# A block's output projection by seven products of quarters, with prepared weights kept in DRAM

## The chip, the cores and the metric

The kernel runs on one core of one Trainium2 chip. The metric is the device time of one execution in microseconds, median of several. TensorE is called PE here, VectorE DVE, ScalarE ACT, GpSimd POOL, and SyncE, which issues nearly all DMAs, SP.

## The reference

One layer on x of 1024 tokens by 1024 channels, all in float32. Two attentions of 8 heads each (a and b) run on one normed input; each is gated, projected to 1024 channels, weighted by its own sigmoid gate, and the sum goes through one output projection that is added to x with a gate per channel:

```python
merged = (jax.nn.sigmoid(mg_a) * (y_a @ w_branch_a[l])
          + jax.nn.sigmoid(mg_b) * (y_b @ w_branch_b[l]))
x = x + gate[:, None, :] * (merged @ w_out[l])
```

`merged` is 1024 x 1024, `w_out` 1024 x 1024; `gate` has one value per output channel and comes from c alone.

## The kernel before

Every product is made in three passes: both operands are split into a high part (rounded, ACT) and a low part (the rest, DVE), and high x high, high x low and low x high are summed in one accumulator (`mm3`, lines 129 to 132). All engines' orders are written by hand: the tile framework keeps program order on each engine and adds the waits. SP's queue is in order too: a DMA that waits holds all that follow.

Places in SBUF are slots of two pools: 29 of 4 KB a partition (`U`) and 11 of 2 KB (`Hs`), handed out oldest first (lines 42 to 72). A slot may be given out while its last readers still run; the new writer then waits for them.

The attention (lines 1239 to 1296) runs 16 heads (0 to 7 branch a, 8 to 15 branch b) of 12 steps each. A step turns one column block of p by PE transposes into a bank `pt` (two banks, shared with the transposes that prepare q and k), ACT casts the high part and DVE takes the low part (lines 1192, 1193), and the product with v is queued for the next step (line 1295). Between them stand the scores of the next blocks (row maximum on DVE, exponential on ACT, scaling by the inverse sum on POOL, lines 1143 to 1178), the preparation of the next pair of heads, a list `extra` of calls at given steps (line 1287), and then filler matmuls (lines 909 to 1013) until PE's planned time of the step is used up. The fillers are the gates' products and, in heads 14 and 15 and after them, the branch products: per 128 channels and 512 tokens 12 matmuls, then DVE's evacuation (lines 984 to 999) to `mA`, whose high and low parts go into `hT_hi` and `hT_lo` as the projection's left operand. One filler chunk's weights are loaded when the chunk before it starts, behind what line 1010 has asked for, and split one unit later.

`w_out` is loaded in two halves of columns (2 MB each): the first when branch a's products end (line 1010), split on ACT and POOL during branch b's (line 1012); the second before `output` and split inside it. `output` (lines 1299 to 1332) makes 16 tiles of 128 tokens x 512 channels, 24 matmuls each; DVE multiplies by the gate row spread over all partitions, adds x, and the tile is stored. The last tile is made in two halves of 256 columns. `gate_row` (line 894) puts the gate into DRAM in head 3.

## Time and profile before

| | us |
|---|---|
| median of 3 runs | 975.56 (973.75 to 977.09) |
| profiled execution | 970.98 |
| its span, first to last instruction | 969.0 |
| attention, heads 4 to 11 | about 428 to 687 |
| branch a's, then b's products end | about 832 and 876 |
| output projection, PE | 877.6 to 965.1 |

The granted TensorE clock was 0.998 of full speed over the span. Busy time of PE counts pipelined matmuls and says when it had work, not its peak rate; a stretch in which PE is busy throughout can get longer only by waits. How far apart matmuls start is the rate.

### The profile page before, as it was taken

The numbers are of one execution on the slowest core, as the hardware profiler recorded it, in microseconds if no ns is written. First come the engines' busy times: TensorE is split into PE (matmuls) and PEld (weight loads), VectorE is DVE, ScalarE is ACT, GpSimd is POOL, SyncE is SP. The second block draws the span as 40 slices with busy tenths as digits, with TensorE's granted clock in tenths as the row PEclk, the third lists the DMA queues.
The fourth block names the chain that finished last, engine by engine and source line by source line (L and its number), as shares of the span: only waits on it lengthen the run. The fifth ranks groups of instructions, "written<-read, shape, count | busy, mean of one in ns | idle before, by whom it ended". The sixth has DMA issues, their size and how long they took to land.

```text
span 969.0 us, 15332 instructions
## 1 busy us (share of the span) xinstructions
PE 952.2 (98%) x5582; PEld 832.3 (86%) x5582; DVE 636.0 (66%) x1379; ACT 477.6 (49%) x959; POOL 204.0 (21%) x260
## 2 busy tenths in 40 slices
PE   7999999999999999999999999999999999999998
PEld 7999999999988888788888888888888878887887
DVE  3967977787646667567667676677676766596222
ACT  7776634443245656546555566465655644143000
POOL 0022132200011222122233233232332220045000
PEclk9999999999999999999999999999999999999999
DMA  9821132864943224225232232322411554633321
GB/s 348 322 95 45 50 116 81 295 225 169 312 134 98 87 67 131 66 74 155 79 109 67 66 90 67 114 85 88 132 56 44 185 185 153 245 141 125 109 88 66
DMA packets 80987, 124.99 MB, mean 129 GB/s; under 512 B 5928, under 2 KB 47536, under 8 KB 80912
## 3 DMA queue, kind: packets, MB, share of 16 engines
q1 hardware_dynamic: 80912, 124.01, 39.3%
q8 instruction: 44, 0.72, 0.3%
q14 instruction: 31, 0.25, 0.1%
HBM read 88.33 MB, written 35.66 MB: 128 GB/s over the span
## 4 chain that ended last, share of the span: by engine, by line
PE 89%; DVE 4%; DMA 3%; ACT 2%; issue 2%; POOL 0%; SPq 0%; ACTq 0%; DVEq 0%
PE f L127 31%; PE b L127 12%; PE out L127 9%; PE s L127 9%; PE o L127 7%; PE pt L136 6%; PE q L127 3%; PE ckv L127 2%; PE kv L127 2%; PE cq_s L127 2%; DVE hT_lo L998 1%; DMA ks_u<-ka_d 1%; PE cq_t L127 1%; DVE mg_h L991 1%; PE pada L127 1%
## 5 line engine op out<-in xcount | busy, mean ns | idle before, releaser
L1192 ACT CAST pp_u<-pt 128x512 fp32r<-128x512 f32 x192 | 92.2, 480 | 178.9 <-PE pt L136 164.9
L1193 DVE TENSOR_TENSOR pp_u<-pt,pp_u 128x512 fp32r<-128x512 f32 x192 | 106.5, 555 | 76.5 <-ACT pp_u L1192 74.4
L127 PE MATMUL f<-hT_hi,hi_f_u 128*128 128x512 f32 x384 | 153.9, 401 | 0.0
L127 PE MATMUL f<-hT_lo,hi_f_u 128*128 128x512 f32 x384 | 153.7, 400 | 0.0
L127 PE MATMUL f<-hT_hi,lo_f_u 128*128 128x512 f32 x384 | 153.5, 400 | 0.0
L127 PE MATMUL s<-k_u,q_u 96*128 96x512 f32 (+6 forms) x480 | 117.1, 363 | 1.2 <-ACT p_h L1172 0.7
L127 PE MATMUL b<-hi_b_u,hT_hi 128*128 128x256 f32 x384 | 109.6, 286 | 0.0
L127 PE MATMUL b<-hi_b_u,hT_lo 128*128 128x256 f32 x384 | 108.6, 283 | 0.0
L127 PE MATMUL b<-lo_b_u,hT_hi 128*128 128x256 f32 x384 | 108.6, 283 | 0.0
L1176 POOL TENSOR_SCALAR p_u<-p_u,rs 128x640 f32<-128x640 f32 (+1 forms) x64 | 64.7, 1011 | 169.1 <-DVE rs L1175 93.2
L1166 DVE TENSOR_REDUCE nm<-s 128x1 f32<-128x128 f32 (+7 forms) x128 | 97.0, 758 | 4.4
L127 PE MATMUL o<-pp_u,v_u 128*128 128x512 f32 (+7 forms) x384 | 94.4, 340 | 0.0
L1176 POOL TENSOR_SCALAR p_h<-p_h,rs 128x128 f32<-128x128 f32 (+1 forms) x64 | 36.9, 577 | 249.3 <-DVE rs L1175 220.0
L127 PEld LDWEIGHTS s<-k_u,q_u 96*128 96x128 f32 (+2 forms) x480 | 77.1, 191 | 7.0 <-ACT p_h L1172 1.2
L127 PEld LDWEIGHTS f<-hT_hi,lo_f_u 128*128 128x128 f32 x384 | 72.5, 189 | 12.0
L127 PEld LDWEIGHTS f<-hT_hi,hi_f_u 128*128 128x128 f32 x384 | 72.7, 189 | 11.1
L127 PEld LDWEIGHTS f<-hT_lo,hi_f_u 128*128 128x128 f32 x384 | 72.5, 189 | 11.2
L127 PEld LDWEIGHTS o<-pp_u,v_u 128*128 128x128 f32 (+1 forms) x384 | 62.0, 162 | 19.7 <-issue 0.2
L127 PEld LDWEIGHTS b<-lo_b_u,hT_hi 128*128 128x128 f32 x384 | 73.6, 192 | 0.3
L127 PEld LDWEIGHTS b<-hi_b_u,hT_hi 128*128 128x128 f32 x384 | 73.6, 192 | 0.3
L127 PEld LDWEIGHTS b<-hi_b_u,hT_lo 128*128 128x128 f32 x384 | 73.6, 192 | 0.0
L136 PEld LDWEIGHTS pt<-ident,p_u 128*128 128x128 f32 x416 | 52.7, 140 | 16.7
(310 smaller groups left out, 1998.5 us busy)
## 6 DMA issues: line engine op xcount, KB each, us to landing
raw_f_u<-in_w_t SPq DMA_DIRECT2D x24, 512.0 KB
wada_u<-in_w_ada SPq DMA_DIRECT2D x16, 512.0 KB
mg_d<-th_h SPq DMA_DIRECT2D x32, 256.0 KB
mg_h<-mg_d SPq DMA_DIRECT2D x32, 256.0 KB
raw_b_u<-in_w_b SPq DMA_DIRECT2D x12, 512.0 KB
x_u<-in_x SPq DMA_DIRECT2D x8, 512.0 KB
raw_wg_u<-in_w_gate SPq DMA_DIRECT2D x8, 512.0 KB
va_d<-vhl_u SPq DMA_DIRECT2D x8, 512.0 KB
```

The source lines that it names most:

```text
L127: self.nc.tensor.matmul(out, lhsT=l, rhs=r, start=start, stop=stop)
L136: self.nc.tensor.transpose(out=out, in_=in_, identity=self.ident)
L991: nc.vector.scalar_tensor_tensor(out=m, in0=m, scalar=1.0, in1=acc, op0=ALU.add, op1=ALU.mult)
L998: nc.vector.tensor_tensor(out=self.hT_lo[x], in0=mA[c1][:, x[2]], in1=self.hT_hi[x].bitcast(F32), op=ALU.subtract)
L1166: nc.vector.tensor_reduce(out=nm, in_=sv, axis=AX.X, op=ALU.max, negate=True)
L1176: nc.gpsimd.tensor_scalar(out=p[:, 0:w], in0=p[:, 0:w], scalar1=rs, scalar2=0.0, op0=ALU.mult, op1=ALU.add)
L1192: nc.scalar.copy(ph[:, c0:], pt[:, c0:])
L1193: nc.vector.tensor_tensor(out=pl[:, c0:], in0=pt[:, c0:], in1=ph[:, c0:].bitcast(F32), op=ALU.subtract)
```

## The change

Operands and result of the output projection are cut into quarters: A11, A12 (channels 0 to 511 and 512 to 1023 of the first 512 tokens), A21, A22 (of the last 512 tokens), and B11 to B22 of `w_out`, already multiplied by the gate. Seven products of quarters (Winograd's form of Strassen's scheme) take the place of eight:

- the left operands are A11, A11 - A21, A12, S2 = S1 - A11, S1 = A21 + A22, A22 and S4 = A12 - S2; the right ones, in the same order, are B11, T3 = B22 - B12, B21, T2 = B22 - B12 + B11, T1 = B12 - B11, T4 = B21 - T2 and B22;
- the four quarters of the result are sums of the products, made on DVE, and x is added; the gate multiplication of the result is gone;
- S1, S2 and S4 are made on DVE from the float32 `mA`, which is now kept, and split into the places of quarters of `hT_hi` and `hT_lo` that are no longer needed. A11 - A21 is made in the branch products, in place of A21 itself (four more DVE steps of 128 x 512).

The right operands are made in heads 4 to 11, one group of rows in each two heads (k = 0 to 3): two loads of 512 KB of `w_out` and one of the gate row at steps 0 and 1, the gate multiplication at steps 4 and 6, and then seven parts, at steps 8 and 10 of the even head and 1, 3, 5, 7, 9 of the odd one. Each part is up to two sums, one cast on ACT, one subtraction on DVE; its high and low parts (256 KB each) are stored to DRAM at the next part. All seven are 14 MB. `wo_load` reads one of them back as four DMAs of 512 KB: 11 and T3 when branch a's products end, the other five during `output`.

```diff
-        low, mA = [], {}
+        low, mA = [], self.mA
...
                     mf = mA[c][:, sl]
                     nc.vector.scalar_tensor_tensor(out=m, in0=m, scalar=1.0, in1=acc, op0=ALU.add, op1=ALU.mult)
                     nc.vector.tensor_tensor(out=mf, in0=mf, in1=m, op=ALU.add)
+                    if sh and c < 4:
+                        mf = Hs.get([P, 512], F32, f"dA{c}")
+                        nc.vector.tensor_tensor(out=mf, in0=mA[c][:, 0:512], in1=mA[c][:, 512:1024], op=ALU.subtract)
                     nc.scalar.copy(self.hT_hi[:, c, sl], mf)
-                    low.append((c, sh))
+                    low.append((c, sh, mf))
                     while len(low) > (pos + 1 < len(todo)):
-                        c1, s1 = low.pop(0)
+                        c1, s1, m1 = low.pop(0)
                         x = (slice(None), c1, slice(s1 * 512, s1 * 512 + 512))
-                        nc.vector.tensor_tensor(out=self.hT_lo[x], in0=mA[c1][:, x[2]], in1=self.hT_hi[x].bitcast(F32),
-                                                op=ALU.subtract)
-                        if s1:
-                            U.put(mA.pop(c1))
+                        nc.vector.tensor_tensor(out=self.hT_lo[x], in0=m1, in1=self.hT_hi[x].bitcast(F32), op=ALU.subtract)
+                        if s1 and c1 < 4:
+                            Hs.put(m1)
...
-                    self.w_out_load(0)
-            if kind == 1 and sh == 1 and c in (2, 3, 4, 5):
-                self.w_out_split(0, c - 2)
...
-    def w_out_split(self, c, k):
-        self.wo[c][k] = self.split(self.wo[c][k], f"wo{c}{k}", engine=self.nc.gpsimd)
...
+    WO = ("11", "21", "22", "T1", "T2", "T3", "T4")
+
+    def gate_bc(self):
+        self.gbc = self.U.get([P, D], F32, "gbc")
+        self.nc.sync.dma_start(self.gbc, self.gate_d.broadcast_to([P, D]))
+
+    def wo_rows(self, k):
+        self.wr = [self.load_w(self.t["w_out"][k + 4 * e], [P, 2, 512], f"wo{k}{e}") for e in range(2)]
+
+    def wo_gate(self, e):
+        self.nc.vector.tensor_tensor(out=self.wr[e], in0=self.wr[e], in1=self.gbc.rearrange("p (a b) -> p a b", a=2),
+                                     op=ALU.mult)
+        if e:
+            self.U.put(self.gbc)
+
+    def wo_store(self):
+        for dst, x in self.wo_pending:
+            self.nc.sync.dma_start(dst, x.bitcast(F32))
+            self.Hs.put(x)
+        self.wo_pending = []
+
+    def wo_part(self, k, name):
+        nc, Hs = self.nc, self.Hs
+        self.wo_store()
+        (b11, b12), (b21, b22) = ((x[:, 0], x[:, 1]) for x in self.wr)
+        tmp = None
+        if name[0] == "T":
+            tmp = Hs.get([P, 512], F32, f"w{name}{k}")
+            a, b = {"T1": (b12, b11), "T3": (b22, b12), "T2": (b22, b12), "T4": (b21, self.t2)}[name]
+            nc.vector.tensor_tensor(out=tmp, in0=a, in1=b, op=ALU.subtract)
+            if name == "T2":
+                nc.vector.tensor_tensor(out=tmp, in0=tmp, in1=b11, op=ALU.add)
+        x = {"11": b11, "21": b21, "22": b22}.get(name, tmp)
+        hi, lo = (Hs.get([P, 512], F32R, f"w{name}{k}{e}") for e in "hl")
+        nc.scalar.copy(hi, x)
+        nc.vector.tensor_tensor(out=lo, in0=x, in1=hi.bitcast(F32), op=ALU.subtract)
+        i = self.WO.index(name)
+        self.wo_pending = [(self.wo_d[i, e, :, k], y) for e, y in enumerate((hi, lo))]
+        if name == "T2":
+            self.t2 = tmp
+        elif tmp is not None:
+            Hs.put(tmp)
+        if name == "T4":
+            Hs.put(self.t2)
+
+    def wo_done(self):
+        self.wo_store()
+        self.U.put(*self.wr)
+
+    def wo_load(self, name):
+        i = self.WO.index(name)
+        out = []
+        for h in range(2):
+            pair = [self.U.get([P, 2, 512], F32R, f"w{e}{name}{h}") for e in "hl"]
+            for e, x in enumerate(pair):
+                self.nc.sync.dma_start(x.bitcast(F32), self.wo_d[i, e, :, 2 * h:2 * h + 2])
+            out.append(pair)
+        self.wo[name] = out
...
+        order = [(st, 0) for st in range(4)] + [(st, 1) for st in range(4, 8)] + [(st, 0) for st in range(4, 8)] + \
+            [(st, 1) for st in range(4)]
...
+        def sum_a(dst, a, b, op):
+            for k in range(4):
+                nc.vector.tensor_tensor(out=dst(k), in0=a(k), in1=b(k), op=op)
+
+        def split_a(src, k0, cols):
+            for k in range(4):
+                nc.scalar.copy(hi[:, k0 + k, cols], src(k))
+            for k in range(4):
+                nc.vector.tensor_tensor(out=lo[:, k0 + k, cols], in0=src(k), in1=hi[:, k0 + k, cols].bitcast(F32),
+                                        op=ALU.subtract)
+
+        s1f = lambda k: mA[k][:, R]
+        s2f = lambda k: mA[k][:, L]
+        s4f = lambda k: mA[4 + k][:, L]
...
+        def banks(tags):
+            out = []
+            for tag in tags:
+                b = self.bank(tag, f"out_{tag}{len(out)}")
+                out += [b[:, 0:512], b[:, 512:1024]] if tag == "s" else [b]
+            return out
+
+        def product(acc, k0, tok, name, ls=slice(0, 512)):
+            for k in range(4):
+                wh, wl = self.wo[name][k // 2]
+                sl = slice(tok * P, (tok + 1) * P)
+                self.mm3(acc[:, ls], hi[:, k0 + k, sl], lo[:, k0 + k, sl], wh[:, k % 2, ls], wl[:, k % 2, ls],
+                         k == 0, k == 3)
+
+        def add(out, a, b):
+            nc.vector.tensor_tensor(out=out, in0=a, in1=b, op=ALU.add)
+
+        def finish(u, acc, other, ls=slice(0, 512)):
+            st, c = order[u]
+            ot = Hs.get([P, 512], F32, f"ot{u}{ls.start}")
+            add(ot[:, ls], acc[:, ls], other[:, ls])
+            add(ot[:, ls], ot[:, ls], xt[u][:, ls])
+            nc.sync.dma_start(t["out"][st * P:(st + 1) * P, c * 512 + ls.start:c * 512 + ls.stop], ot[:, ls])
+            Hs.put(ot)
+            if ls.stop == 512:
+                Hs.put(xt.pop(u))
+                load(u + 4)
...
-        for u in range(2 * ST):
-            c, st = divmod(u, ST)
-            if u + 3 < 2 * ST:
-                load(u + 3)
-            if c == 0 and 2 <= st < 6:
-                self.w_out_split(1, st - 2)
-            sl = slice(st * P, (st + 1) * P)
-            ot = Hs.get([P, 512], F32, f"ot{u}")
-            x, n = xt.pop(u), 2 if u == 2 * ST - 1 else 1
-            for e in range(n):
-                ls = slice(e * 512 // n, (e + 1) * 512 // n)
-                cs = slice(c * 512 + ls.start, c * 512 + ls.stop)
-                acc = self.bank("ttof"[(u + e) % 4], f"out{u}{e}")[:, ls]
-                for k in range(KT):
-                    wh, wl = self.wo[c][k // 2]
-                    self.mm3(acc, self.hT_hi[:, k, sl], self.hT_lo[:, k, sl], wh[:, k % 2, ls], wl[:, k % 2, ls],
-                             k == 0, k == KT - 1)
-                nc.vector.tensor_tensor(out=ot[:, ls], in0=acc, in1=gbc[:, cs], op=ALU.mult)
-                nc.vector.tensor_tensor(out=ot[:, ls], in0=ot[:, ls], in1=x[:, ls], op=ALU.add)
-                nc.sync.dma_start(t["out"][st * P:(st + 1) * P, cs], ot[:, ls])
-            Hs.put(ot, x)
...
+        self.wo_load("21")
+        X = banks("nsg")
+        s1s, s1 = four("p1_")
+        for i in range(4):
+            product(X[i], 0, i, "11")
+            nc.scalar.copy(s1[i], X[i])
+            if i == 0:
+                self.wo_load("T2")
+                sum_a(s1f, s1f, lambda k: mA[4 + k][:, R], ALU.add)
+            if i == 1:
+                sum_a(s2f, s1f, s2f, ALU.subtract)
+        done("11")
+        self.wo_load("T1")
+        split_a(s2f, 0, L)
+        Z = banks("ttof")
+        a7s, a7 = four("a7_")
+        for i in range(4):
+            product(Z[i], 0, 4 + i, "T3")
+            add(a7[i], Z[i], s1[i])
+            if i == 0:
+                sum_a(s4f, s4f, s2f, ALU.subtract)
+        done("T3")
+        self.wo_load("T4")
+        split_a(s1f, 0, R)
+        for k in range(4):
+            U.put(mA.pop(k))
+        X = banks("nsg")
+        for i in range(4):
+            product(X[i], 4, i, "21")
+            finish(i, X[i], s1[i])
+        done("21")
+        self.wo_load("22")
+        split_a(s4f, 4, L)
+        for k in range(4, 8):
+            U.put(mA.pop(k))
+        Z = banks("ttof")
+        es, e = four("e_")
+        for i in range(4):
+            product(Z[i], 0, i, "T2")
+            add(s1[i], Z[i], s1[i])
+            add(e[i], Z[i], a7[i])
+        X = banks("nsg")
+        for i in range(4):
+            product(X[i], 0, 4 + i, "T1")
+            add(s1[i], X[i], s1[i])
+            finish(4 + i, X[i], e[i])
+        Z = banks("ttof")
+        for i in range(4):
+            product(Z[i], 4, 4 + i, "T4")
+            finish(8 + i, Z[i], e[i])
+        X = banks("nsg")
+        for i in range(4):
+            n = 2 if i == 3 else 1
+            for h in range(n):
+                ls = slice(h * 512 // n, (h + 1) * 512 // n)
+                product(X[i], 4, i, "22", ls=ls)
+                finish(12 + i, X[i], s1[i], ls)
...
+        self.wo_d = dp.tile([7, 2, P, 4, 512], F32, name="wo_d")
...
+            n = 4 + 2 * k
+            self.extra += [((n, 0), self.wo_rows, (k,)), ((n, 1), self.gate_bc, ()), ((n, 4), self.wo_gate, (0,)), ((n, 6), self.wo_gate, (1,))]
+            self.extra += [((n + i, s), self.wo_part, (k, name)) for i, s, name in (
+                (0, 8, "T3"), (0, 10, "11"), (1, 1, "T2"), (1, 3, "T4"), (1, 5, "T1"), (1, 7, "21"), (1, 9, "22"))]
+            self.extra += [((n + 1, 11), self.wo_done, ())]
...
-            self.w_out_load(1)
...
-    o["w_out"] = np.stack([np.stack([_chunks(a["w_out"][0][256 * k:256 * (k + 1), 512 * c:512 * (c + 1)], 2)
-                                     for k in range(4)]) for c in range(2)])
+    o["w_out"] = np.ascontiguousarray(a["w_out"][0].reshape(8, P, 2, 512))
```

`finish` adds two results and x and stores the tile; `split_a` casts four blocks on ACT and subtracts on DVE; `product` is 12 matmuls of one token block.

## Rows read from the trace of the kernel before

**Rows 1.** The page, part 1: busy time, share of the span, instructions

```profile
PE 952.2 (98%) x5582; PEld 832.3 (86%) x5582; DVE 636.0 (66%) x1379; ACT 477.6 (49%) x959; POOL 204.0 (21%) x260
```

**Rows 2.** Busy time by stretch, heads 4 to 11; last three: clock, DMA share, GB/s

```profile
428.00:460.00 32.00, 32.00 (x179) 27.02 (x178) 23.34 (x48) 20.30 (x43) 6.97 (x9) 1.00 0.45 123
...
sum 259.00, PE 258.75 PEld 215.90 DVE 177.81 ACT 151.59 POOL 75.84; mean PE 32.34 PEld 26.99 DVE 22.23 ACT 18.95 POOL 9.48
```

**Rows 3.** PE's waits from 260 to 877 us: total us, times, longest

```profile
PE kt L136 <- DMA ks_u<-ka_d: 1.6, 1, 1.6
```

**Rows 4.** The chain that ended last, its close: start, us, engine, tile

```profile
877.60 87.66 PE out L127 x408
...
965.29 0.44 DVE ot_h L1329
...
965.75 0.43 DVE ot_h L1330
```

**Rows 5.** The timeline of PE, projection's first matmul: start, us, [idle before]

```profile
877.60 0.50 PE L127 MATMUL out<-hi_wo_u,hT_hi 128*128 128x512 f32 x1 [1.68 <-DVE mg_h L991]
```

**Rows 6.** The timeline of PE, the last two matmuls

```profile
964.85 0.28 PE L127 MATMUL out<-lo_wo_u,hT_hi 128*128 128x256 f32 x1
964.97 0.28 PE L127 MATMUL out<-hi_wo_u,hT_lo 128*128 128x256 f32 x1
```

**Rows 7.** The tile ot: min/median/max ns of one, first and last start

```profile
L1329 DVE TENSOR_TENSOR ot_h<-out,gbc_u x17: 425/692/692, 883.4 to 965.3; 128x512 f32<-128x512 f32 x15, 128x256 f32<-128x256 f32 x2
L1330 DVE TENSOR_TENSOR ot_h<-ot_h,xo_h x17: 426/692/1715, 884.1 to 965.7; 128x512 f32<-128x512 f32 x15, 128x256 f32<-128x256 f32 x2
```

**Rows 8.** Busy time by stretch, two microseconds of the branch products

```profile
838.00:840.00 2.00, 2.00 (x11) 1.65 (x10) 0.00 (x0) 0.00 (x0) 0.00 (x0) 1.00 1.00 352
```

**Rows 9.** The timeline of SP's queue, end of the first branch

```profile
826.21 7.29 SPq L102 DMA_DIRECT2D raw_wo_u<-in_w_out  x4
...
833.55 0.42 SPq L102 DMA_DIRECT2D raw_f_u<-in_w_br  x1
```

**Rows 10.** The timeline of ACT, same stretch

```profile
840.24 1.14 ACT L115 CAST hi_f_u<-raw_f_u 128x512 fp32r<-128x512 f32 x2 [3.01 <-DMA raw_f_u<-in_w_br]
```

**Rows 11.** The timeline of PE, first use of that weight

```profile
843.13 0.39 PE L127 MATMUL f<-hi_y_u,hi_f_u 128*128 128x512 f32 x1
```

**Rows 12.** The timeline of DVE, the low part alone and beside POOL

```profile
853.04 0.69 DVE L998 TENSOR_TENSOR hT_lo<-mA_u,hT_hi 128x512 fp32r<-128x512 f32 x1
...
854.97 1.78 DVE L998 TENSOR_TENSOR hT_lo<-mA_u,hT_hi 128x512 fp32r<-128x512 f32 x1
```

**Rows 13.** Groups by line, 831 to 885 us: count, busy us, mean ns

```profile
L998 DVE TENSOR_TENSOR hT_lo<-mA_u,hT_hi 128x512 fp32r<-128x512 f32 x16 | 15.3, 958 | 0.1
...
L116 POOL TENSOR_TENSOR lo_wo_u<-raw_wo_u,hi_wo_u 128x512 fp32r<-128x512 f32 x11 | 17.8, 1645 | 68.3 <-DVE mg_h L991 55.3 <-ACT hi_wo_u L115 11.2 <-issue 1.9
```

**Rows 14.** Groups by line and form, 400 to 700 us: filler splits

```profile
L116 DVE TENSOR_TENSOR lo_f_u<-raw_f_u,hi_f_u 128x512 fp32r<-128x512 f32 x30 | 20.7, 730 | 1.3 <-ACT hi_f_u L115 1.3
...
L115 ACT CAST hi_f_u<-raw_f_u 128x512 fp32r<-128x512 f32 x30 | 17.1, 622 | 0.1
```

**Rows 15.** The timeline by engine, head 9, steps 1 to 4

```profile
593.33 1.23 DVE L1166 TENSOR_REDUCE nm<-s 128x1 f32<-128x1024 f32 x1
...
596.68 0.42 DVE L1193 TENSOR_TENSOR pp_u<-pt,pp_u 128x256 fp32r<-128x256 f32 x1
...
596.12 1.13 ACT L1172 ACTIVATE p_u<-s,nm 128x1024 f32<-128x1024 f32 x1
...
597.86 1.13 POOL L1176 TENSOR_SCALAR p_u<-p_u,rs 128x1024 f32<-128x1024 f32 x1 [5.30 <-PE pt L136]
...
597.35 0.60 PE L136 MATMUL kt<-ident,ks_u 128*128 128x128 f32 x4
...
598.95 0.40 PE L127 MATMUL o<-pp_u,v_u 128*128 128x256 f32 x2
...
599.65 0.60 PE L136 MATMUL pt<-ident,p_u 128*128 128x128 f32 x4
```

More of the change, by code (lines that the diff above doesn't have):

```diff
@@ L1009, in fillers @@
                         U.put(*self.y[kk])
-                    self.w_out_load(0)
-            if kind == 1 and sh == 1 and c in (2, 3, 4, 5):
-                self.w_out_split(0, c - 2)
+                    self.wo_load("11")
+                    self.wo_load("T3")
             yield 1300. if kind == "t" and c < 8 else 1000.
-    def w_out_load(self, c):
-        self.wo[c] = [self.load_w(self.t["w_out"][c, k], [P, 2, 512], f"wo{c}{k}") for k in range(4)]
-    def w_out_split(self, c, k):
-        self.wo[c][k] = self.split(self.wo[c][k], f"wo{c}{k}", engine=self.nc.gpsimd)
+    WO = ("11", "21", "22", "T1", "T2", "T3", "T4")
@@ L1300, in output @@
         nc, t, Hs, U = self.nc, self.t, self.Hs, self.U
-        gbc = U.get([P, D], F32, "gbc")
-        nc.sync.dma_start(gbc, self.gate_d.broadcast_to([P, D]))
+        mA, hi, lo = self.mA, self.hT_hi, self.hT_lo
+        L, R = slice(0, 512), slice(512, 1024)
         xt = {}
+        order = [(st, 0) for st in range(4)] + [(st, 1) for st in range(4, 8)] + [(st, 0) for st in range(4, 8)] + \
+            [(st, 1) for st in range(4)]
         def load(u):
-            c, st = divmod(u, ST)
-            xt[u] = Hs.get([P, 512], F32, f"xo{u}")
-            nc.sync.dma_start(xt[u], t["x"][st * P:(st + 1) * P, c * 512:(c + 1) * 512])
@@ L1310, in output @@
-        for u in range(3):
-            load(u)
-        for u in range(2 * ST):
-            c, st = divmod(u, ST)
-            if u + 3 < 2 * ST:
-                load(u + 3)
-            if c == 0 and 2 <= st < 6:
-                self.w_out_split(1, st - 2)
-            sl = slice(st * P, (st + 1) * P)
-            ot = Hs.get([P, 512], F32, f"ot{u}")
-            x, n = xt.pop(u), 2 if u == 2 * ST - 1 else 1
-            for e in range(n):
-                ls = slice(e * 512 // n, (e + 1) * 512 // n)
-                cs = slice(c * 512 + ls.start, c * 512 + ls.stop)
-                acc = self.bank("ttof"[(u + e) % 4], f"out{u}{e}")[:, ls]
-                for k in range(KT):
-                    wh, wl = self.wo[c][k // 2]
-                    self.mm3(acc, self.hT_hi[:, k, sl], self.hT_lo[:, k, sl], wh[:, k % 2, ls], wl[:, k % 2, ls],
-                             k == 0, k == KT - 1)
-                nc.vector.tensor_tensor(out=ot[:, ls], in0=acc, in1=gbc[:, cs], op=ALU.mult)
-                nc.vector.tensor_tensor(out=ot[:, ls], in0=ot[:, ls], in1=x[:, ls], op=ALU.add)
-                nc.sync.dma_start(t["out"][st * P:(st + 1) * P, cs], ot[:, ls])
-            Hs.put(ot, x)
@@ new lines, in load, with four @@
+            if u < 16:
+                st, c = order[u]
+                xt[u] = Hs.get([P, 512], F32, f"xo{u}")
+                nc.sync.dma_start(xt[u], t["x"][st * P:(st + 1) * P, c * 512:(c + 1) * 512])
+        def four(name):
+            pair = [U.get([P, 2, 512], F32, f"{name}{i}") for i in range(2)]
+            return pair, [pair[i // 2][:, i % 2] for i in range(4)]
+        def sum_a(dst, a, b, op):
+            for k in range(4):
+                nc.vector.tensor_tensor(out=dst(k), in0=a(k), in1=b(k), op=op)
@@ new lines, in product @@
+        def product(acc, k0, tok, name, ls=slice(0, 512)):
[7 more added lines that the diff above has]
+        def finish(u, acc, other, ls=slice(0, 512)):
+            st, c = order[u]
+            ot = Hs.get([P, 512], F32, f"ot{u}{ls.start}")
[6 more added lines that the diff above has]
+                load(u + 4)
@@ new lines, in done @@
+        def done(name):
+            for pair in self.wo.pop(name):
+                U.put(*pair)
+        for u in range(4):
+            load(u)
+        self.wo_load("21")
[9 more added lines that the diff above has]
+                sum_a(s2f, s1f, s2f, ALU.subtract)
@@ L1363, in build @@
         self.passes, self.qk, self.v, self.p, self.gates, self.y, self.wo = {}, {}, {}, {}, {}, {}, {}
+        self.mA, self.wo_pending, self.t2 = {}, [], None
         self.extra = []
@@ L1370, in build @@
         self.extra += [((3, 0), self.gate_row, ())]
+        for k in range(4):
+            n = 4 + 2 * k
[3 more added lines that the diff above has]
+            self.extra += [((n + 1, 11), self.wo_done, ())]
         with tc.manual_schedule():
```

## The prediction

> **What bounds the kernel now.** The shares of busy time say that TensorE is the bound nearly everywhere: PE is busy 98% of the span, DVE 66%, ACT 49%, POOL 21% [rows 1]. The change touches two stretches. The first is heads 4 to 11 of the attention, about 428 to 687 us, where PE has 258.75 us of work in 259, DVE 177.81 (69%), ACT 151.59 (59%), and DMA moves some 90 GB/s [rows 2]. PE never waits there for long: in the list of PE's waits its longest one behind a DMA is 1.6 us, once [rows 3]. So each microsecond that anything holds PE here is added to the end. The second stretch is the end. The chain of waits closes with 87.66 us of PE on the output projection, 408 matmuls without a break, and then two DVE steps and the last store [rows 4]. The projection begins after PE sat 1.68 us for DVE [rows 5], since its first accumulator takes a bank that DVE must still empty. Everything that the change saves is in this second stretch; everything that it pays for is in the first one and between the two.
>
> **The products.** Before, 16 tiles take 24 matmuls each, the last in two halves: 360 of 512 columns and 48 of 256. Half-width ones start 0.12 us apart [rows 6]. From 877.60 to the end of the last one, 965.09, that leaves (87.49 - 48 x 0.12)/360 = 0.227 us for a full one. After, seven products of four tiles take 12 each: 28 x 12 = 336, of which 324 are full and 24 half. That is 36 x 0.227 + 24 x 0.12 = 8.17 + 2.88 = 11.05 us less.
> The Trainium skill (TensorE: Matmul & The Clock Gate, section Back-to-back issue gap) gives about 131 ns for a 512-column matmul in a sustained stream. By it 48 full equivalents would be worth only 6.3 us, an estimate, and the end would come 4.8 us later than I sum here. The trace does not agree: 0.227 us in this very loop, so the row is used.
>
> **Can the other engines follow the shorter stage?** A tile now takes PE 12 x 0.227 = 2.72 us instead of 5.45. DVE no longer multiplies by the gate, but has 12 sums of operands, 12 subtractions for the low parts and about 50 sums on results. The busiest products (T3, 21, T2, T1) put 12 of these on DVE, 12 x 0.69 us (the median of today's pair on a result tile, [rows 7]) = 8.3 us in 10.9. Three operands are resplit in place, and each has at least one whole other product (10.9 us) between the last read of the old value and the first read of the new one: eight instructions, ACT and DVE in parallel, some 4 us. Of weights, 5 x 2 MB must still come in while some 55 us of products run, along with 4 MB of x and 4 MB of output: some 250 GB/s over 76 us, and today the queues reach 352 GB/s when full [rows 8]. Every set is asked for at least two products ahead. I cost this at nothing; its cover is the order of the products, and if it is gone the price is up to a product's worth of saving, 5 us. The last tile has both halves in one accumulator, where two were used: 0 to 1 us, I take 0, because the readers touch other columns.
>
> **The start of the projection.** The first tile goes into a bank that the attention left long ago, its weights are loaded a stage earlier, and its operand (rows 0 to 3, first half of the tokens) is final early. So the 1.68 us of [rows 5] goes: -1.7. What is late next is DVE's queue behind it, used only by the sums for the fourth product, 30 us later.
>
> **The load queue between attention and projection.** In the branch products the weights of the projection are asked for when the first branch ends, ahead of the next filler's weights. SP issues four of them from 826.21 to 833.50, most of that time held by slots that PE lets go of at the end of the branch; the filler's own load is out at 833.55 [rows 9]. It lands behind them: the queue runs at 352 GB/s [rows 8], and ACT can split only from 840.24 [rows 10]. Its first half is used by PE at 843.13 [rows 11], and both parts are ready some 2.1 us before that (ACT's two casts take 1.14 together; DVE's low half follows). After, eight loads stand there instead of four (11 and T3, high and low): 4 x 0.52 MB more at 352 GB/s is 6.0 us, less 2.1 of slack, with 0.5 of it taken back because the queue is not yet full in its first microsecond: PE stalls about 3.4 us. Bounds: 0 if slots or queue let the filler's load pass, 6 if the slack goes too. I take 3.4, as the sizes and the order are plain from the code. Behind it DVE is 5 us late, and has four more subtractions (4 x 0.69). But it gets back what POOL took: the low-part subtraction takes 0.69 us alone and 1.78 beside POOL's weight split [rows 12], and those splits are gone (today the mean of its 16 is 0.958 [rows 13]). So it ends about where it does now, some 3 us behind PE, inside the cover of the first product.
>
> **Heads 4 to 11.** For each of four row groups: two loads (1 MB), the gate row spread over all partitions (0.5 MB), two gate multiplications of 1024 columns, 12 DVE steps of 512 (5 sums or differences and 7 low parts), 7 casts on ACT, 14 stores. Priced by today's split of filler weights, 0.730 us on DVE and 0.622 on ACT for the same shapes [rows 14]: DVE 4 x (12 + 2 x 2) x 0.730 = 46.7 us, to 224.5 of 259 (87%); ACT 28 x 0.622 = 17.4 us, to 65%. All of it lies beside PE, as long as it makes no step of a head late. DMA gets 21 MB more, about 81 GB/s, half the queue in all. The stores stand on SP's queue in front of the loads of q, k, v and fillers, but each is issued a part later (two steps, 5.4 us) than its value, so SP stands where the heads already are; these loads have three steps or more until use. I cost them at nothing; if that cover goes, the nearest row is the 1.6 us of [rows 3] each time.
> What can be late is read from a step of an odd head, where the costliest insert (T2, three DVE steps around one cast) goes right behind the widest row maximum (593.33). Head 9 is the tightest of its kind [rows 15]: POOL has the last block of p ready at 598.99, PE turns it at 599.65 (0.66 spare); DVE ends the low part of that step at 597.10, PE uses it at 599.07 (2.0 spare), but the transposes of k at 597.35 need the same bank (0.25 spare). T2 takes 3 x 0.73 us of DVE plus 0.62 for the cast between; some 1.2 us of DVE idle time absorb a part, and I see 1 to 1.5 us late. In heads 5, 7 and 11 only the bank is tight, some 0.5 us each. Other inserts are one to two DVE steps with about 2 us spare. Sum: 1.5 + 3 x 0.5 = 3.0. Bounds: 0 (all absorbed) and 13 (each of the 36 inserts, 28 parts and 8 gate steps, holds PE for half of one DVE step, 0.36 us). I take 3, as the rows are nearer to it.
>
> **Sum.** -11.05 - 1.7 + 3.4 + 3.0 = -6.35. The profiled execution took 970.98 us, 4.6 under the median of 975.56; on it the sum gives 964.6, on the median 969.2.
>
> **Rivals.** (a) Fully covered: the filler's load is not held up or the heads hide everything. For it: the 2 us or more of spare in most steps; against: one queue, in order. With -12.75 + 0 to 3.4: 962.8 to 966.2, middle 965. (b) DVE at 87% stutters: the inserts hold PE for some 10 us. For it: 0.25 us spare at the bank; against: DVE's lag has two steps to go away. 975.56 - 9.35 + 10 = 976.2, no change. (c) Slower, by the port that DVE and POOL fight for. Beside POOL's two-input subtraction the same DVE step takes 1.78 us, not 0.69, and all 48 inserted steps and 8 multiplications read two SBUF tiles while POOL scales p for 75.84 of 259 us [rows 2, 12]. If DVE and POOL hold each other for whole instructions, p is late and the heads wait. Price: 56 steps x 0.29 chance x 1.1 us = 18 us, if none is hidden: 975.56 - 9.35 + 18 = 984. It decides from 12.3 us held in the heads (0.34 per insert). Against it: the filler splits run among the same POOL work and average 0.730 [rows 14].
> The Trainium skill (SBUF — State Buffer, section Who interferes with whom) says that a DVE instruction with two SBUF inputs and a GpSimd instruction that reads SBUF lock each other out for the whole instruction. The 1.78 us agrees; the 0.730 says that it is met seldom or hidden.
> (d) The change doesn't give what it says: DVE or the weight loads set the pace of the seven products and half of the 11 is lost: 974.7.
>
> **How the numbers follow.** Forecast 0.50 (966.2 to 972.6); (a) 0.20; (b) 0.16; (c) 0.09; (d) 0.05. About 0.3% (2.9 us) is what a measurement of this kernel can tell from no change, so faster is below 972.6: 0.50 + 0.20 = 0.70; same: 0.16 + 0.05 = 0.21; slower: 0.09. The range takes in (a) to its end and (b) with its spread: 963 to 977.
>
> **What the profile will show.** If right: 336 matmuls on the projection in 76.4 us without waits inside; no wait at its start; a PE wait of 2 to 5 us near 843 that ends with ACT or DVE on the filler's weights, these behind a DMA; in heads 4 to 11 DVE at 85 to 88% and small PE waits, mostly in odd heads at steps 2 to 4, together under 6 us. Wrong if the projection shows waits for DVE or DMA between its products, if PE waits for loads of q, k or v, or if the 259 us of the eight heads grow by more than 6.

## The result, and the profile after

The changed kernel takes 996.89 us (993.91 to 998.8, 4 runs) against 974.74 (973.75 to 977.09, 4 runs): a ratio of 1.0237 [1.021, 1.0264], slower by some 2.4% where 969.2 had been forecast. Its profiled execution has a span of 992.1 us, 23.1 more than before.

The page's busy times of the kernel after, in the form of [rows 1]:

```profile
PE 952.9 (96%) x5522; PEld 825.0 (83%) x5522; DVE 692.9 (70%) x1479; ACT 493.0 (50%) x987; POOL 185.6 (19%) x244
```

PE has 60 matmuls less and is as long busy as before, in a longer span: what the products save is lost elsewhere. By stages of the span, read between the same instructions in both traces (ACT's first cast of a turn in head 4 and in head 12, the last branch matmul, the first and last matmul of the projection):

| us | before | after | difference |
|---|---|---|---|
| up to head 4 | 428.4 | 430.8 | +2.4 |
| heads 4 to 11 | 258.3 | 279.5 | +21.2 |
| head 12 to the last branch matmul | 188.8 | 195.8 | +7.0 |
| from there to the projection's first | 2.06 | 0.23 | -1.8 |
| projection, first to last start | 87.4 | 81.8 | -5.6 |

The first line isn't the change's: kernels below with the same work there begin head 4 anywhere from 426.1 to 432.1 us.

Heads 4 to 11, the sum by stretch that answers to [rows 2]:

```profile
sum 279.47, PE 265.36 PEld 215.91 DVE 215.83 ACT 165.78 POOL 82.45; mean PE 265.36 PEld 215.91 DVE 215.83 ACT 165.78 POOL 82.45
```

PE is idle for 14.1 us, and DVE, at 77%, is far from full. All of PE's waits in these heads (us in total, times, longest; before had one of 0.2 us here):

```profile
PE kt L136 <- DVE pp_u L1249: 7.2, 6, 2.1
PE s L127 <- ACT p_u L1228: 2.1, 2, 1.9
PE s L127 <- ACT p_h L1228: 1.8, 4, 0.7
PE pt L136 <- DVE pp_u L1249: 1.5, 3, 0.6
PE o L127 <- DVE pp_u L1249: 0.6, 1, 0.6
PE qt L136 <- DVE pp_u L1249: 0.5, 2, 0.3
```

No wait is for a DMA. Together they are 13.7 us; set against the starts of the same matmuls in the kernel before, a wait costs PE 0.16 to 0.27 us more than the idle time listed (1.44 for the 1.27 of the first `kt` below). Half of it is one kind: the transposes of k (`kt`) need a bank that DVE must still empty (the low part of p, `pp`). How that comes about is seen in head 4, step 8, where the part T3 stands. The timeline of the kernel after by engine (DVE, ACT, PE; start, us):

```profile
455.71 0.67 DVE L1047 TENSOR_TENSOR wT_h<-raw_wo_u,raw_wo_u 128x512 f32<-128x512 f32 x1
457.07 0.69 DVE L1053 TENSOR_TENSOR wT30l_h<-wT_h,wT30h_h 128x512 fp32r<-128x512 f32 x1 [0.69 <-ACT wT30h_h L1052]
458.07 1.29 DVE L116 TENSOR_TENSOR lo_f_u<-raw_f_u,hi_f_u 128x512 fp32r<-128x512 f32 x2 [0.31 <-ACT hi_f_u L115]
459.29 0.55 DVE L1249 TENSOR_TENSOR pp_u<-pt,pp_u 128x384 fp32r<-128x384 f32 x1
...
456.42 0.62 ACT L1052 CAST wT30h_h<-wT_h 128x512 fp32r<-128x512 f32 x1 [1.47 <-DVE wT_h L1047]
457.44 1.12 ACT L115 CAST hi_f_u<-raw_f_u 128x512 fp32r<-128x512 f32 x2
...
459.89 0.66 PE L136 MATMUL kt<-ident,ks_u 128*128 128x128 f32 x4 [1.27 <-DVE pp_u L1249]
```

and the same place in the kernel before:

```profile
453.97 0.55 DVE L1193 TENSOR_TENSOR pp_u<-pt,pp_u 128x384 fp32r<-128x384 f32 x1
...
454.68 0.60 PE L136 MATMUL kt<-ident,ks_u 128*128 128x128 f32 x4
```

Before, the low part ended 0.16 us ahead of the transposes. The part puts a sum, an idle 0.69 us in which DVE stands until ACT has cast, and a subtraction into DVE's order: 2.05 us where 0.16 could be spared. ACT pays too: its cast waited 1.47 us for the sum with the filler's cast behind it, and DVE then waited 0.31 for that one. In the odd heads it is T2, with two sums. Head 5, kernel after:

```profile
471.96 0.68 DVE L1047 TENSOR_TENSOR wT_h<-raw_wo_u,raw_wo_u 128x512 f32<-128x512 f32 x1
472.68 0.69 DVE L1049 TENSOR_TENSOR wT_h<-wT_h,raw_wo_u 128x512 f32<-128x512 f32 x1
474.06 0.69 DVE L1053 TENSOR_TENSOR wT20l_h<-wT_h,wT20h_h 128x512 fp32r<-128x512 f32 x1 [0.69 <-ACT wT20h_h L1052]
474.67 0.42 DVE L1249 TENSOR_TENSOR pp_u<-pt,pp_u 128x256 fp32r<-128x256 f32 x1
...
475.14 0.66 PE L136 MATMUL kt<-ident,ks_u 128*128 128x128 f32 x4 [1.04 <-DVE pp_u L1249]
```

Between the end of branch a and the projection PE waits once, for the filler's weights, which stand behind the eight loads of 11 and T3 on SP's queue (SP, ACT, PE; compare [rows 9 to 11]):

```profile
850.75 0.32 SPq L1073 DMA_DIRECT2D wh_u<-wo_d  x1
...
859.93 0.73 SPq L1073 DMA_DIRECT2D wlT_u<-wo_d  x1
860.70 0.65 SPq L102 DMA_DIRECT2D raw_f_u<-in_w_br  x1
...
871.31 1.14 ACT L115 CAST hi_f_u<-raw_f_u 128x512 fp32r<-128x512 f32 x2 [9.53 <-DMA raw_f_u<-in_w_br]
...
871.98 0.74 PE L127 MATMUL f<-hi_y_u,hi_f_u 128*128 128x512 f32 x1 [4.14 <-ACT hi_f_u L115]
872.52 0.63 PE L127 MATMUL f<-lo_y_u,hi_f_u 128*128 128x512 f32 x1
872.94 0.63 PE L127 MATMUL f<-hi_y_u,lo_f_u 128*128 128x512 f32 x1
```

In the projection PE waits for readers of accumulators, all but one time at `out_s`, the bank pair that holds two of the four tiles of a product (PE's waits from head 12 to the end; then DVE and PE at one of them):

```profile
PE out_s L127 <- DVE ot_h L1406: 2.9, 3, 1.4
...
PE out_s L127 <- ACT p_u L1430: 0.7, 1, 0.7
PE out_g L127 <- DVE ot_h L1406: 0.5, 1, 0.5
```

```profile
934.74 0.69 DVE L1406 TENSOR_TENSOR ot_h<-out_s,p_u 128x512 f32<-128x512 f32 x1 [1.01 <-PE out_s L127]
...
935.48 0.50 PE L127 MATMUL out_s<-wh_u,hT_hi 128*128 128x512 f32 x1 [0.78 <-DVE ot_h L1406]
```

The second half's matmuls, 935.48, start when DVE's read of the first half, at 934.74 for 0.69 us, is over, although they write other columns.

### The profile page after: what moved, and what is told of

The parts are those of the page before. It is cut to its first block, busy times and chain, and to the rows that moved or that the text cites. A ratio compares the mean times of both kernels' runs of the same rounds, so it can differ in the third digit from the quotient of the medians.

```text
span 992.1 us, 15503 instructions
## 1 busy us (share of the span) xinstructions
PE 952.9 (96%) x5522; PEld 825.0 (83%) x5522; DVE 692.9 (70%) x1479; ACT 493.0 (50%) x987; POOL 185.6 (19%) x244
## 4 chain that ended last, share of the span: by engine, by line
PE 76%; DVE 9%; ACT 6%; DMA 4%; issue 4%; SPq 1%; POOL 0%; ACTq 0%; DVEq 0%
PE f L127 26%; PE b L127 12%; PE s L127 7%; PE o L127 5%; PE pt L136 5%; PE q L127 3%; PE out_s L127 2%; PE ckv L127 2%; PE kv L127 2%; PE cq_s L127 2%; DVE pp_u L1249 2%; PE out_t L127 2%; DVE nm L1222 2%; DMA raw_f_u<-in_w_br 2%; PE out_g L127 1%
## 5 line engine op out<-in xcount | busy, mean ns | idle before, releaser
L1232 POOL TENSOR_SCALAR p_h<-p_h,rs 128x128 f32<-128x128 f32 (+1 forms) x64 | 42.3, 662 | 254.1 <-DVE rs L1231 226.7
L127 PEld LDWEIGHTS f<-hT_hi,hi_f_u 128*128 128x128 f32 x384 | 73.0, 190 | 11.2
L127 PEld LDWEIGHTS o<-pp_u,v_u 128*128 128x128 f32 (+1 forms) x384 | 62.0, 162 | 21.2 <-DVE pp_u L1249 1.4
L1228 ACT ACTIVATE p_u<-s,nm 128x640 f32<-128x640 f32 (+1 forms) x64 | 61.5, 961 | 17.1 <-DVE nm L1222 13.0
```

The source lines that it names most:

```text
L127: self.nc.tensor.matmul(out, lhsT=l, rhs=r, start=start, stop=stop)
L1228: nc.scalar.activation(p[:, 0:w], sv, AF.Exp, bias=nm, accum_out=sm)
L1232: nc.gpsimd.tensor_scalar(out=p[:, 0:w], in0=p[:, 0:w], scalar1=rs, scalar2=0.0, op0=ALU.mult, op1=ALU.add)
```

## The experiments

All kernels below are the changed one with the edit shown. Stage times are read as in the table above, each from one execution: the same heads read 279.5, 280.5 and 281.0 (after, e5, e6), and 269.0 and 272.8 where DVE waits long (e3, e7). Ratios are to the kernel before on the same chip.

| kernel | heads 4 to 11 | 12 to last branch matmul | projection | time, ratio |
|---|---|---|---|---|
| before | 258.3 | 188.8 | 87.4 | 1 |
| after | 279.5 | 195.8 | 81.8 | 996.89, 1.0237 [1.021, 1.0264] |
| e1_heads_empty | 258.3 | 194.6 | 81.8 | 971.5, 0.9987 [0.9965, 1.001] |
| e2_heads_dma_only | 259.5 | 195.6 | 81.8 | 973.53, 1.0009 [0.9987, 1.0031] |
| e4_no_round_trip | 271.1 | 196.5 | 81.8 | 984.24, 1.0108 [1.0076, 1.014] |
| e8_split_in_place | 267.1 | 197.0 | 81.8 | 981.46, 1.0085 [1.0051, 1.0119] |
| e5_filler_first | 280.5 | 188.5 | 81.8 | 987.79, 1.016 [1.0127, 1.0193] |
| e6_banks | 281.0 | 196.2 | 76.2 | 986.16, 1.0156 [1.0123, 1.0188] |
| e3_placed | 269.0 | 198.1 | 81.8 | 982.73, 1.0113 [1.0078, 1.0148] |
| e7_all | 272.8 | 189.9 | 76.2 | 971.57, 0.9995 [0.9974, 1.0016] |
| e9_placed_late_gate | 265.3 | 196.3 | 81.8 | 979.2, 1.0067 [1.0045, 1.009] |
| e10_all_late_gate | 265.6 | 191.0 | 76.2 | 968.6, 0.9946 [0.9926, 0.9965] |
| e11_slots_only | 260.0 | 197.3 | 81.8 | 973.67, 0.9999 [0.9975, 1.0024] |
| e12_gate_halves | 265.9 | 190.2 | 76.2 | 968.98, 0.9959 [0.9936, 0.9983] |
| e13_rows_after_store | 261.1 | 189.7 | 76.2 | 961.36, 0.9911 [0.988, 0.9942] |
| e14_store_raw | 259.8 | 189.3 | 76.2 | 962.55, 0.9902 [0.988, 0.9924] |

**Work or transfers in the heads?** The first kernel drops everything in heads 4 to 11, and the second keeps its loads and stores alone.

```diff
-        self.extra += [((n, 0), self.wo_rows, (k,)), ((n, 1), self.gate_bc, ()), ...]
```

> Leaves out all work on the projection's weights in heads 4 to 11 (loads, gate, sums, casts, stores); the projection reads other data of the same size from DRAM, so its output is not the reference's. After took 279.5 us for these heads, before 258.3. Every theory that puts the loss there expects 258 to 260 and, on the median, 997 - 21 = 976; what is then left between this kernel and before (975) is the projection's gain and the filler's stall. If the heads stay over 265, the loss has another cause.

```diff
     def wo_part(self, k, name):
         self.wo_store()
+        self.wo_pending = [(self.wo_d[i, e, :, k], self.wr[e][:, i % 2]) for e in range(2)]
-        ...sums, cast, subtraction
```

> Keeps the loads, the gate row's load and the 56 stores in heads 4 to 11 at their steps, with raw data, and leaves out every DVE and ACT instruction of the parts (the output is not the reference's). Theory A (sum, cast and low part in line hold DVE's and ACT's queues) and theory B (DVE's load of 87% as such): heads at 258 to 261, median about 976 to 978. Theory C (traffic and slots: stores ahead of loads in SP's queue, fewer free slots): heads over 270, median over 988.

Heads 4 to 11 take 258.3 and 259.5 us, the latter with DVE and ACT as busy as before, by the same view as above:

```profile
sum 259.48, PE 258.50 PEld 215.22 DVE 177.68 ACT 151.67 POOL 75.79; mean PE 258.50 PEld 215.22 DVE 177.68 ACT 151.67 POOL 75.79
```

So 21 MB of transfers cost 1.2 us, and 20 of the 21.2 us come with the work on DVE and ACT. With the work the second kernel also leaves out the small slots that the parts take and the waits of their stores for late results; the last experiments bear on these.

**Its amount, or the wait across engines inside a part?** One kernel keeps every instruction, but the cast and the subtraction read operands that lie ready (what is stored is then not the high and low parts). The other keeps the data and splits each part over steps, sum, cast and low part each a step or so apart, near the old places.

```diff
-        nc.scalar.copy(hi, x)
-        nc.vector.tensor_tensor(out=lo, in0=x, in1=hi.bitcast(F32), op=ALU.subtract)
+        nc.scalar.copy(hi, b11)
+        nc.vector.tensor_tensor(out=lo, in0=x, in1=b12, op=ALU.subtract)
```

> All instructions of the parts stay where they are, with the same shapes, but the cast reads a row block instead of the sum and the low part subtracts a row block instead of the high part, so that neither engine waits for the other inside a part (the output is not the reference's). Theory A: without the wait DVE loses 0.7 us less a part and ACT's queue is not blocked; heads at 262 to 269. Theory B (load alone): as after, 276 to 280. Theory D (the steps themselves: no idle time of DVE before the next use, with or without the wait): 272 to 280 as well, so B and D are told apart by the next run but one.

```diff
-        (0, 8, "T3"), (0, 10, "11"), (1, 1, "T2"), (1, 3, "T4"), ...
+        (8,0,'wo_sum','T3'),(9,0,'wo_cast','T3'),(10,0,'wo_low','T3'),(10,0,'wo_cast','11'),...
+        (13,0,'wo_sum','T2'),(14,0,'wo_cast','T2'),(15,0,'wo_low','T2'),(15,0,'wo_sum','T4'),...
```

> The same instructions as after, each part started at the same step, but its cast is issued one step after the sum and the low part one step after the cast, so that both inputs are long there; results as after. Theory A (the wait inside a part): heads at 260 to 268, median 977 to 986. Theory B (DVE's load of 87%): unchanged, 276 to 280, median about 995. Theory D (steps where DVE has no idle time): between, some 268 to 275.

Sum of the heads and PE's waits for `kt`, first without the wait across engines, then split:

```profile
sum 271.15, PE 262.52 PEld 214.72 DVE 217.96 ACT 167.07 POOL 82.45; mean PE 262.52 PEld 214.72 DVE 217.96 ACT 167.07 POOL 82.45
...
PE kt L136 <- DVE pp_u L1249: 3.6, 6, 1.0
```

```profile
sum 267.06, PE 261.25 PEld 214.85 DVE 215.69 ACT 166.60 POOL 88.97; mean PE 261.25 PEld 214.85 DVE 215.69 ACT 166.60 POOL 88.97
...
PE kt L136 <- DVE pp_u L1264: 0.3, 1, 0.3
```

With DVE as busy (216 to 218 us), 8.3 and 12.4 us go: for these the work's place and order count, not its amount. Taking the wait away halves `kt`'s (7.2 to 3.6), though at 271.1 the heads stay above the 262 to 269 expected of that alone; with single steps 0.3 is left. POOL's busy time also speaks against the port of rival (c): it is longest, 88.97, where the loss is small.

**The filler's weights and the banks.** The loads of 11 and T3 are asked for behind the loads of the next filler chunks; the halves of `out_s` are made second and last, so that the tile in `out_g` lies between them, and the last half tile has a bank of its own.

```diff
-                    self.wo_load("11")
-                    self.wo_load("T3")
...
                 load_mg(todo[pos + 1][1])
+            if start and kind == 1 and c in (0, 2):
+                self.wo_load(("11", "T3")[c // 2])
```

> As after, but the loads of 11 and of T3 are each asked for behind a filler's weights (at the start of the first and of the second filler of branch b) and not ahead of them. If the 4.3 us wait of PE for the filler's weights and the slow matmuls behind it come from the loads' order in the queue: the stretch from head 12 to the last branch matmul falls from 195.8 to 189 to 191 us, median 990 to 992. If it came from anything else (slots, DVE's sums), it stays at 194 or more.

```diff
         X = banks("nsg")
+        X = [X[0], X[1], X[3], X[2]]
...
+                acc = X[i] if h == 0 else self.bank("o", "out_last")
```

> As after, but the two tiles that share the double accumulator s are not made one after the other (a tile in g stands between), and the last tile's second half has a bank of its own. If PE's waits of 0.8 to 1.5 us before each third tile are the wait for the reader of the other half: the projection falls from 81.8 to 76.4 to 77.5 us, median about 992. If DVE's pace is the cause: it stays above 80.

Each removes its loss and leaves the other stages as they were: 195.8 to 188.5 (PE's wait for an exponential, 1.2 us in the kernel after, is 0.2 here too), and 81.8 to 76.2 us, with no wait left in the projection.

**Placing every step by hand.** The same micro-steps at steps where the trace of before had idle time on DVE, those marked with a 1 early in the step; then that together with the two edits above.

```diff
+        (3,1,'wo_gate',0,0),(5,1,'wo_gate',0,1),(6,0,'wo_gate',1,0),(7,0,'wo_gate',1,1),(8,0,'wo_cast','11'),
+        (10,1,'wo_low','11'),(10,1,'wo_sum','T3'),...,(12,0,'wo_cast','T3'),(14,0,'wo_low','T3'),...
```

> The same instructions as after and the same results. Each DVE step of a part stands alone, at a step of the heads where DVE's rows of the kernel before show an idle gap of half a microsecond or more ahead of its next due work (even heads 3, 5, 6, 7, 10; odd heads 2, 3, 5 to 8, 10, 11), the casts and low parts each later than their inputs. With the parts split but at their old steps the heads took 267.1 us, with no DVE or ACT work 259.5. If the steps' idle time decides (theory D): heads at 259 to 263, median 974 to 979. If DVE's load as such decides (theory B): 266 to 268, median about 981.

> The three changes together, results as after. From the runs so far: heads at 259 to 263, 189 to 191 from head 12 to the last branch matmul, projection at 76.4 to 77.5. Against before (258.3, 188.8 + 2.1, 87.4) that is -11.0 - 1.8 + 1 to 5 + 0 to 2, a median of 962 to 967, ratio 0.989 to 0.994. If the slots or the queue get in the way when all three meet, some stretch stays at its old length.

269.0 us, worse than the plain split, and all three together 0.9995 with 272.8 us in the heads: both miss what was expected (259 to 263 us, and 0.989 to 0.994). The list of DVE's waits in the first names the largest loss:

```profile
DVE raw_wo_u L1031 <- DMA gbc_u<-gate_d: 12.4, 4, 3.9
```

The first gate multiplication, put early into step 3, stood up to 3.9 us for the gate row, with the head's own work behind it. With the row asked for at step 0 and the first product at step 5 (the steps of T3 and of 22 also move three or four steps back, so that what is gained is not the gate row's alone):

```diff
+        (0,0,'gate_bc'),(5,1,'wo_gate',0,0),(6,0,'wo_gate',0,1),(7,0,'wo_gate',1,0),...,(10,1,'wo_gate',1,1),...,
+        (14,0,'wo_sum','T3'),...,(15,0,'wo_cast','T3'),...,(18,0,'wo_low','T3'),...,(21,0,'wo_cast','22'),...,(22,0,'wo_low','22'),...
```

> As the run with the parts placed in idle gaps, but the gate row is asked for one step earlier and the first gate multiplication stands two steps later. In that run DVE waited 3.9, 12.4 us in all, for the gate row's load that had been issued 6 us earlier, with the preparation of q behind it, and all of PE's loss lay in the even heads. If that wait was what kept the heads at 269.0: heads at 259 to 262, median 973 to 976. If DVE's load as such is left (theory B): 266 to 268.

> The same together with the fillers' loads first and the accumulators' order; results as after. Heads at 259 to 262, 188 to 190 from head 12 to the last branch matmul, projection at 76.2: against before -11.2 - 1.8 + 1 to 4 + 0 to 1, a median of 961 to 965 beside before's 973, ratio 0.988 to 0.993. If the DVE load of the heads cannot be hidden, no better than 968.

265.3 and 265.6 us, and with the other two edits 0.9946 [0.9926, 0.9965]. DVE no longer waits for the gate row, but both miss the 259 to 262 expected and come near what DVE's load as such was to give (266 to 268). Some 7 us are left. The largest waits stand at the start of heads 8 and 10; one of them, placed kernel (PE, ACT, SP):

```profile
569.21 0.65 PE L136 MATMUL pt<-ident,p_u 128*128 128x128 f32 x4 [1.30 <-DVE pp_u L1264]
...
568.56 0.27 ACT L1263 CAST pp_u<-pt 128x128 fp32r<-128x128 f32 x1 [3.38 <-DMA ya_d<-op_u]
...
555.69 0.32 SPq L1076 DMA_DIRECT2D wo_d<-w221l_h  x1
...
559.62 0.33 SPq L1022 DMA_DIRECT2D gbc_u<-gate_d  x1
562.74 0.33 SPq L1294 DMA_DIRECT2D ya_d<-op_u  x1
```

The cast waits for a slot whose store is on its way, behind the last stores, the rows and the gate row.

**Slots, work or queue?** First the slots: one kernel holds them all and leaves the work out (raw rows are stored), one takes the gate row out of the pool of large slots.

```diff
-        self.nc.sync.dma_start(self.wo_d[i, e, :, self.k], x.bitcast(F32))
+        self.nc.sync.dma_start(self.wo_d[i, e, :, self.k], self.wr[e][:, i % 2])
-        ...all sums, casts, products
```

> The placed version with the late gate, with its loads, its stores (of the raw rows of w_out) and every slot held as long as there, but without any of the work on DVE and ACT, so its projection gets wrong weights. The placed version takes 265.3 us in heads 4 to 11, 7 more than without the work (258.3); the one with DMA alone and the gate slot held for 5 steps 259.5. Theory A, the rest of the loss is slots (one more slot of the large pool held for ten steps lets new tiles meet slots whose stores are still on their way): 263 to 266. Theory B, it is the place of the work on DVE and ACT: 258.5 to 260.5.

```diff
-        self.gbc = self.U.get([P, D], F32, "gbc")
+        self.gbc = [self.Hs.get([P, 512], F32, f"gb{h}") for h in range(2)]
```

> The fastest version so far (work placed, gate late, filler's weights first, banks apart; 265.6 us in heads 4 to 11, 0.9946 of the time before) with the gate row loaded as two halves into the pool of small slots, not one large slot; the multiplications go half by half, so that each half is let go after two. If the held large slot is behind the rest of the loss: heads 4 to 11 at 260 to 263 and some 964 us in all; if it is not: 265 to 267 and 968 to 969.

260.0 and 265.9: the large slots are not it. But the first of these also freed SP, whose stores no longer waited for a low part, and the small slots, which its stores no longer read; so it could not tell work from queue, as its expectation had assumed. The last two do: one moves rows and gate row behind the head's store, one keeps all the work and stores the raw rows.

```diff
-        (0,0,'wo_rows'),(0,0,'gate_bc'),
+        (2,0,'wo_rows'),(2,0,'gate_bc'),
```

> The fastest version so far (265.6 us in heads 4 to 11, 0.9946) with the two loads of rows and the gate row moved from step 0 to step 2 of the even head, behind the store of the head's result and the load of v on SP's queue. If the queue is behind the rest of the loss (2.5 MB of last stores, rows and gate stand in front of that store, and ACT, q and the turns of p wait for slots that it holds): the waits at the start of heads 8 and 10 go, heads 4 to 11 take 261 to 263, in all 964 to 966. If it is the place of the work on DVE and ACT: 265 to 267 and 968 to 970.

> The same fastest version, all work on DVE and ACT in its place, but the stores take the rows of w_out that have lain ready for long in place of the high and low parts (so the projection's weights are wrong): SP never stands behind a low part, and all bytes stay. With the slots and DMA alone heads 4 to 11 took 260.0, with the work 265.6. If SP standing behind late low parts is the rest of the loss: 260 to 262. If the place of the work on DVE and ACT is: 264 to 266. A burst of transfers in itself, whatever they wait for: 264 to 266 here, and the kernel beside it falls.

261.1 and 259.8 us: 4.5 and 5.8 of the 7 us go with what stands on SP's queue, and DVE's load as such is ruled out, since its work is all there. The first is the cleaner of the two: its stores are unchanged, while in the second they also let the small slots go early. (It takes its large slots two steps later, too; e11 and e12 speak against these.) With the rows moved the sum of the heads and PE's waits in them are:

```profile
sum 261.11, PE 259.21 PEld 215.13 DVE 217.88 ACT 166.29 POOL 86.31; mean PE 259.21 PEld 215.13 DVE 217.88 ACT 166.29 POOL 86.31
...
PE s L127 <- ACT p_u L1243: 0.8, 2, 0.7
PE qt L136 <- DVE pp_u L1264: 0.5, 2, 0.3
PE kt L136 <- DVE pp_u L1264: 0.5, 1, 0.5
```

The 2.8 us by which these heads are still longer than before stay open. That kernel takes 961.36 us, 0.9911 [0.988, 0.9942] of the time before: the seven products do pay once their preparation is placed and the filler's loads and the accumulators are put right.

## Why the prediction was wrong

**The step that failed: heads 4 to 11, 3.0 us taken, bounds 0 to 13, measured 21.2.** Three things in it were wrong.
- "Other inserts are one to two DVE steps with about 2 us spare": this was read from head 9 alone. At the `kt` of heads 4, 6 and 8, behind T3, the spare time was 0.16, 0.19 and 1.25 us. By the growth of PE's delay over the kernel before, T3 cost 1.44, 1.45 and 0.53 us there, where nothing had been counted.
- "Some 1.2 us of DVE idle time absorb a part": too much. T2's length was as forecast (2.78 us in head 9 for 2.81), but of the idle time only 0.91 us lay on DVE's way to `kt`, and that way grew by 2.11 us (2.54 to 4.65 from the row maximum's end), so that 0.7 were absorbed. T2 cost 2.25 us at `kt` in head 9 (1 to 1.5 forecast), and 1.20 and 1.32 in heads 5 and 7 (0.5 each). DVE's free 31% were an average, and the wait for ACT inside a part made a further 0.69 us of idle time that nothing else could use.
- The cost was counted on DVE's way to `kt` alone. A part also stands in ACT's order (the 1.47 us in head 4), and 3.9 us of the waits are of the scores (`s`) for late exponentials on ACT; how the parts made each of these late wasn't traced.

The six steps at `kt` add up to 8.2 us. Of the other 13, some 10 are waits at `s`, `pt`, `o` and `qt`, counted in the same way, 1.6 a slower clock (below), and the rest is spread thinly. The amount of the work was no part of it: DVE's busy time grew by 38.0 us (177.81 to 215.83) where 46.7 had been priced. The upper bound, half a DVE step for each of 36 inserts, was no bound: it left out the wait across engines, and one insert could cost three steps. Without that wait the loss was 12.8, just inside it.

**Transfers in the heads, nothing taken: nearly right.** 1.2 us with DMA alone. But in that kernel no store waits for a sum, a cast or a low part, so it doesn't test "SP stands where the heads already are". In the placed kernel that was wrong: the order on SP's queue was worth 4.5 us (265.6 to 261.1), with 1.1 to 1.4 each for the three largest waits, near the price of [rows 3] that was named for a lost cover. How much of the 21.2 us it makes in the kernel after isn't shown.

**Filler's load, 3.4 us taken, bounds 0 to 6, measured 4.1 of wait, 5.8 in all.** Place, order and releaser were as forecast (PE for ACT for the DMA). SP's eight loads were issued from 850.75 to 860.66, held by slots for 6 us of it, and the filler's landed 10.6 us after its issue. What the sum left out is what follows the wait: matmuls 0.427 us apart, not 0.227, until 875.5, some 1.7 us. (The stage's other 1.2 us is one wait of PE for an exponential in its heads.)

**Projection: products right, the accumulator wrong.** With banks that don't wait, it takes 76.2 us for 76.4 forecast, -11.2 for -11.05: the 0.227 us of [rows 6] held, and the 131 ns that the Trainium skill gives (TensorE: Matmul & The Clock Gate, section Back-to-back issue gap) did not. DVE and the weights followed without a wait, as taken. But "the readers touch other columns" was wrong: the writer of one half waited for the reader of the other, in the last tile (0.5 us idle, 0 to 1 allowed) and also, where nothing had been counted, once in each of the four products that use the double accumulator `out_s` (3.6 us idle). With what each wait costs beyond its idle time that makes 5.6 us.

**Start: right.** 1.8 for 1.7, and no wait took its place.

**Rivals.** The sign was that of (c), and its condition, 12.3 us held in the heads, was met; its mechanism showed in four steps only. 44 of the 48 added steps of 512 columns ran in 0.67 to 0.69 us; the four T1 sums took 1.21 (below), 2.1 us more in all. POOL's busy time rose by 6.6 us (75.84 to 82.45) and by more, 13.1, in the split kernel, which loses less than half. The lock between DVE and POOL that the Trainium skill states (SBUF — State Buffer, section Who interferes with whom) agrees with those four sums and may be in the 6.6 us; no wait of PE in these heads is for POOL, and none of the six at `kt` stands behind a T1 sum. (b), DVE that stutters (10 us), came nearest: PE did wait for DVE at the bank, but by the place of the steps, not by the 87% (77% was measured), and for twice as long. The probabilities gave slower 0.09: too little, since what was known of the heads was one head's steps.

## What to carry to other kernels

Work hidden beside a full engine is paid for step by step: before inserting it, list for every step what the next instruction of the bound engine waits for and how much it has to spare, not the mean load of the engine that takes the work. A sum, a cast and a subtraction on two in-order engines should go into separate steps, so that neither stands for the other; and what they store must not stand on a queue ahead of what the bound engine needs soon. Two tiles that follow each other should not share an accumulator, even in different columns.

## What the runs showed of the hardware

The clock falls after waits of PE, though not after each. In head 11 PE waited 1.94 us, in head 9 2.1 (busy time by stretch behind either wait, 614.30 and 677.20, the number after POOL's being the granted clock; then PE behind 677.19):

```profile
614.30:617.00 2.70, 2.70 (x18) 2.34 (x18) 1.06 (x5) 1.97 (x7) 1.98 (x3) 1.00 0.03 6
...
677.20:680.60 3.40, 3.40 (x9) 2.67 (x10) 2.83 (x6) 1.02 (x2) 1.02 (x1) 0.55 0.28 50
```

```profile
678.81 0.63 PE L127 MATMUL f<-hT_hi,hi_f_u 128*128 128x512 f32 x1
679.24 0.63 PE L127 MATMUL f<-hT_lo,hi_f_u 128*128 128x512 f32 x1
...
680.94 0.40 PE L127 MATMUL f<-hT_hi,lo_f_u 128*128 128x512 f32 x1
681.17 0.38 PE L136 MATMUL pt<-ident,p_h 128*128 128x128 f32 x2
```

Behind the one at 677.19 full matmuls start 0.43 us apart until 680.94 and the clock is at its lower level, 1.2 GHz (0.55 over the stretch); behind the one at 614.22 it stays at 1.00, 2.4 GHz. The 4.1 us wait for the filler had the same price as the first. So a wait of 2 us can cost PE nearly twice its length, which no bound of the prediction held; what decides between the two wasn't tried.

DVE was at times held beside POOL. Each of the four T1 sums, which read two blocks of one tile, took 1.21 or 1.22 us where the other added steps of that size took 0.67 to 0.69; it began while POOL's product `op_u` ran and ended half a microsecond behind it (head 5 of the kernel after):

```profile
484.98 1.21 DVE L1047 TENSOR_TENSOR wT_h<-raw_wo_u 128x512 f32<-128x512 f32 x1
...
484.36 1.29 POOL L1278 TENSOR_TENSOR op_u<-op_u,gate_u 128x512 f32<-128x512 f32 x1 [4.49 <-DVE op_u L1272]
```
